# A two-layer encoder on one core: the output projection by blocks, its norm applied late, gates ahead of the next inputs

## The chip, the cores and the metric

The kernel runs as one program on 1 core of a Trainium2 chip. The metric is device time in microseconds (us). The kernel before took 3183.21 us, the median of 3 runs (3179.08 to 3185.33). Engines: PE (TensorE, matmuls), DVE (VectorE), ACT (ScalarE), POOL (GpSimd), SP (SyncE, which here only issues transfers between DRAM and the core's memory, SBUF). PE writes into PSUM banks.

## The reference

A hybrid encoder of two layers (model width 1024, feed-forward width 2816) over a prompt of 256 and a sample of 1024 tokens; 16 meta tokens precede each. All data are float32.

```python
def trunk(x, ...):
    h = concatenate([meta, x], axis=1)
    for layer in range(2):
        hn = rmsnorm(h, norm_mix_g[layer])
        if layer == 0: h = h + ab_layer(hn, ...)        # S5 and RG-LRU halves, concatenated, then @ w_out_ab
        else:          h = h + windowed_gqa(hn, ...)    # +-128 window, 16 heads, then @ w_o
        h = h + conv_ffn(rmsnorm(h, norm_ffn_g[layer]), w_up[layer], ..., w_down[layer])
    return rmsnorm(h, final_norm_g)[:, N_META:]

def conv_ffn(h, w_up, conv_w, conv_b, w_down):
    u = dwconv(h @ w_up, conv_w, conv_b, 1)             # centred, width 3
    a, g = u[..., :D_FF], u[..., D_FF:]
    return (gelu(g) * a) @ w_down
```

## The kernel before

Both sequences, 272 and 1040 tokens with their meta tokens, lie side by side as columns, with a few zero columns between; the 1024 features lie on the 128 partitions in KD = 8 blocks. A float32 matmul is made of three: each operand is split into a high part (`whi`, `hh`: an ACT cast) and the rest (`wlo`, `hl`: a subtraction on DVE or POOL), and `mm3` (L237 to L253) sums high by high, high by low and low by high over the 8 feature blocks. A weight block is `unit` (L226): one 512 KB load into a `raw` tile, the ACT cast, the subtraction.

Stages, in the order of the span: the mixer of layer 0 (to 488 us), `project_out(0)` (488 to 649), `ffn(0)` (649 to 1600), attention of layer 1 with its projections (1600 to 2112), `project_out(1)` (2112 to 2174), `ffn(1)` and the final norm (2174 to 3184).

`project_out` (L1481) works in 4 column chunks of 328 or 330 columns. In layer 0 it takes one chunk after the other and within it the 8 blocks m of output features: 24 matmuls over `hh` and `hl`, and extra matmuls with an identity (L252) that add the residual rows of x, which SP has loaded into `xr` tiles (up to 128 rows of 4 KB). The ACT copy puts the sum into `ha` (chunks 0, 1) or `hb` (2, 3). A chunk's columns of `od` (output of the mixer in DRAM) are staged (`stage`, L1441) through 3 buffers with the tag "t": load, ACT cast to `hh` (L1469), DVE subtraction to `hl` (L1470). Four weight units are kept. Then the norm of the chunk: `square` (8 squares on ACT, 7 adds on DVE at L272), `factors` (PE sums over partitions, L279), `spread` (DVE L289, PE L292), `apply` (8 scalar_tensor_tensor on DVE, L1503); for chunks 2 and 3 the result is stored to `ysp`. In layer 1 attention has handled the blocks of chunks 0 and 1 itself (`out_block`, L1428, over `hr` tiles, which share the tag "t"); at its end `rows(99)` stages everything that is left before the remaining blocks run.

`ffn` (L298) splits w_up into a Strassen-Winograd scheme of 7 products. The columns go in two halves (s = 0, 1). For pairs j of feature tiles PE runs 7 products of 12 matmuls (L427) with weights made of sums of `raw` tiles (POOL, L335) that are split again (ACT L361, POOL L362), and with inputs X1 to X7, sums of quarters of the normed columns (`inputs`, L370: DVE L382, L383, POOL L386, L387; splits at L1478 on ACT, L1479 on DVE). `follow` combines products on DVE (L438 to L449), `convolve` (L394) applies the depthwise taps, `gate` (L472) does gelu, product and split (`xa`, L477, L478). After two pairs, `down` (L490) multiplies by w_down (split at L486, L487; added into `hs` at L497). Between the halves the last pair's gates have to pass before `down` of that pair, and the inputs of the second half are made: here called the half-switch (1109 to 1160 us in layer 0, 2657 to 2690 in layer 1). The order of PE inside `ffn` is written out by hand (`run_pair`, orders SEVEN and TURNS); every other engine's order is set by a scheduler that follows priorities in program order and estimated readiness.

Of the kernel before, what the change touches and what calls it, by code (L numbers as in the profile page):

```python
# [89 lines left out]
class Trunk:  # L90
# [32 lines left out]
    def setup(self):  # L123
# [14 lines left out]
        self.ysp = self.dram.tile([128, KD, W - HALF], F32, tag="ysp", name="ysp")  # L138
# [116 lines left out]
    def norm(self, chunks, h):  # L255
# [4 lines left out]
        tile = lambda tag, n, b=1: p.tile([128, CH + 2], F32, tag=tag, name=tag, bufs=b)[:, :n]  # L260
        st = {}

        parts = lambda n: [min(x, n - 110) for x in range(0, n, 110)]

        def square(c):
            n = chunks[c][1]
            acc = st[c] = tile("acc", n)
            nc.scalar.activation(out=acc, in_=h(c, 0), func=AF.Square)
            for k in range(1, KD):
                sq = tile("t", n, 3)  # L270
                nc.scalar.activation(out=sq, in_=h(c, k), func=AF.Square)
# [26 lines left out]
    def ffn(self, l, p_norm, hn, h1, right):  # L298
# [9 lines left out]
        p_factors, p_spread, p_apply = p_norm  # L308
# [6 lines left out]
        order = lambda j: TURNS if turns(j) else SEVEN  # L315
# [54 lines left out]
        def inputs(first, ya, yb, n):  # L370
# [1327 lines left out]
```

## Time and profile before

| | |
|---|---|
| median of 3 runs | 3183.21 us (3179.08 to 3185.33) |
| the profiled execution | 3185.81 us, span 3184.0 us |
| PE busy | 2836.6 us (89%), 17944 matmuls |
| POOL, DVE, ACT busy | 1718.7 (54%), 2045.2 (64%), 1518.9 us (48%) |
| chain that ended last | PE 68%, DVE 13%, DMA 7%, ACT 4%, POOL 3%, issue 3% |

The span is the time from the first to the last instruction that the profile holds; the execution's own time is 1.81 us longer. In the strip of 40 slices PE stands at 9 in the long middle parts of both feed-forward stages and falls at the borders of stages: slices 7 to 8 (project_out(0), ffn(0) start), 14, 20, 26 to 28 and 33 to 34. The windows below take those borders one by one.

### The profile page before, as it was taken

Reading aid. Unit: us, or ns where it says so; the run is one execution under the profiler, and the core shown is the slowest. Engines: PE = TensorE matmul, PEld = TensorE weight load, DVE = VectorE, ACT = ScalarE, POOL = GpSimd, SP = SyncE. Lnnn points to the kernel's source line nnn. Section 1 sums busy time; section 2 is a strip of 40 time slices with the busy share of each in tenths; the row PEclk is TensorE's granted clock in tenths of the full one; section 3 lists DMA queues with packets and bytes.
Section 4 is the critical chain, followed back from the end, with each engine's and each line's share of the span. In section 5 each row is a group of like instructions: output and inputs, shape, how many; then the busy total and the mean of one; then the engine's idle time right before and its main releaser. Section 6 shows DMA issues by size and latency. Waiting matters only on the chain.

```text
span 3184.0 us, 48855 instructions
## 1 busy us (share of the span) xinstructions
PE 2836.6 (89%) x17944; PEld 2724.3 (86%) x17944; DVE 2045.2 (64%) x4215; ACT 1518.9 (48%) x2921; POOL 1718.7 (54%) x1446
## 2 busy tenths in 40 slices
PE   6999748869999979999979998866899997999996
PEld 5988537869999979999978887866799997899996
DVE  8998793365556685555664777656555556655664
ACT  5445772334444454444434666533444443544442
POOL 1000100078888887888604334316788887788881
PEclk9999878979999989999989999988899998999998
DMA  5322534433222242222237667663422222422221
GB/s 145 88 79 57 132 94 120 125 126 109 80 80 79 77 149 74 80 80 80 84 100 173 132 141 175 147 187 117 141 80 80 80 80 77 133 80 80 80 67 54
DMA packets 413438, 329.78 MB, mean 104 GB/s; under 512 B 39502, under 2 KB 388606, under 8 KB 413198
## 3 DMA queue, kind: packets, MB, share of 16 engines
q1 hardware_dynamic: 359086, 264.15, 28.8%
q0 software_dynamic: 35520, 32.89, 5.2%
q10 hardware_dynamic: 18592, 29.61, 2.7%
q8 instruction: 142, 2.33, 0.3%
q14 instruction: 98, 0.80, 0.1%
HBM read 261.96 MB, written 62.52 MB: 102 GB/s over the span
## 4 chain that ended last, share of the span: by engine, by line
PE 68%; DVE 13%; DMA 7%; ACT 4%; POOL 3%; issue 3%; SPq 1%; DVEq 0%; ACTq 0%; POOLq 0%
PE ps_a L427 9%; PE ps_c L427 9%; PE ps_d L427 9%; PE ps_b L427 5%; PE ps_a L248 4%; PE ps_a L253 4%; PE ps_a L249 4%; PE ps_c L248 2%; PE ps_c L253 2%; PE ps_c L249 2%; PE ps_b L248 2%; PE ps_b L253 2%; PE ps_d L248 2%; PE ps_d L253 2%; PE ps_b L249 2%
## 5 line engine op out<-in xcount | busy, mean ns | idle before, releaser
L487 POOL TENSOR_TENSOR dl<-rawd,dh 128x1024 fp32r<-128x1024 f32 x88 | 213.2, 2423 | 316.0 <-ACT dh L486 316.0
L248 PE MATMUL ps_a<-hh,whi 128*128 128x438 f32 (+5 forms) x848 | 295.7, 349 | 67.3 <-DVE hr L1438 29.9
L486 ACT CAST dh<-rawd 128x1024 fp32r<-128x1024 f32 x88 | 92.1, 1047 | 446.4 <-PE ps_d L249 425.3
L249 PE MATMUL ps_a<-hl,whi 128*128 128x438 f32 (+5 forms) x848 | 291.3, 344 | 1.9 <-DVE hl L1470 1.3
L253 PE MATMUL ps_a<-hh,wlo 128*128 128x438 f32 (+5 forms) x848 | 290.4, 343 | 0.0
L335 POOL TENSOR_TENSOR s<-raw 128x512 f32<-128x512 f32 x184 | 247.6, 1347 | 20.3 <-PE ps_d L253 14.8
L362 POOL TENSOR_TENSOR whi<-s,whi 128x512 fp32r<-128x512 f32 x176 | 234.2, 1341 | 27.6 <-ACT whi L361 27.5
L362 POOL TENSOR_TENSOR wlo<-s,wlo 128x512 fp32r<-128x512 f32 x176 | 234.1, 1331 | 12.5 <-ACT wlo L361 11.7
L248 PEld LDWEIGHTS ps_a<-hh,whi 128*128 128x128 f32 x848 | 165.8, 196 | 78.3 <-DVE hr L1438 30.1
L362 POOL TENSOR_TENSOR whi<-raw,whi 128x512 fp32r<-128x512 f32 x132 | 174.7, 1325 | 83.9 <-ACT whi L361 83.9
L361 ACT CAST wlo<-s 128x512 fp32r<-128x512 f32 x176 | 108.7, 620 | 231.8 <-PE ps_a L427 93.0
L427 PE MATMUL ps_a<-x,wlo 128*128 128x332 f32 (+1 forms) x1056 | 179.0, 319 | 41.6 <-POOL wlo L362 22.9
L427 PEld LDWEIGHTS ps_a<-x,wlo 128*128 128x128 f32 x1056 | 166.6, 192 | 43.0 <-POOL wlo L362 23.8
L427 PE MATMUL ps_d<-x,wlo 128*128 128x332 f32 (+1 forms) x1056 | 177.2, 317 | 6.9 <-ACT wlo L361 6.4
L427 PE MATMUL ps_a<-x,whi 128*128 128x332 f32 (+1 forms) x1056 | 177.8, 318 | 6.0 <-ACT u L436 6.0
L427 PE MATMUL ps_c<-x,wlo 128*128 128x332 f32 (+1 forms) x1056 | 178.4, 319 | 1.6 <-DVE t L443 1.6
L427 PE MATMUL ps_c<-x,whi 128*128 128x332 f32 (+1 forms) x1056 | 179.3, 320 | 0.0
L427 PE MATMUL ps_d<-x,whi 128*128 128x332 f32 (+1 forms) x1056 | 178.0, 318 | 0.0
L427 PEld LDWEIGHTS ps_a<-x,whi 128*128 128x128 f32 x1056 | 166.5, 191 | 6.5 <-ACT u L436 6.5
L362 POOL TENSOR_TENSOR wlo<-raw,wlo 128x512 fp32r<-128x512 f32 x132 | 172.0, 1321 | 0.0
L249 PEld LDWEIGHTS ps_a<-hl,whi 128*128 128x128 f32 x848 | 165.7, 195 | 7.4 <-DVE hl L1470 1.6
L427 PEld LDWEIGHTS ps_d<-x,wlo 128*128 128x128 f32 x1056 | 165.4, 190 | 7.6 <-ACT wlo L361 6.7
(499 smaller groups left out, 8872.9 us busy)
## 6 DMA issues: line engine op xcount, KB each, us to landing
raw<-in_w_up SPq DMA_DIRECT2D x176, 512.0 KB
rawd<-in_w_down SPq DMA_DIRECT2D x88, 512.0 KB
raw<-in_w_o SPq DMA_DIRECT2D x24, 512.0 KB
qs<-st SPq DMA_DIRECT2D x48, 219.0 KB
raw<-in_w_out_ab SPq DMA_DIRECT2D x20, 512.0 KB
q<-qs POOLq DMA_DIRECT2D x80, 128.0 KB, 3.8
hs<-hsp SPq DMA_DIRECT2D x6, 1312.0 KB
raw<-in_w_in_ab SPq DMA_DIRECT2D x12, 512.0 KB
```

The lines of the kernel that those rows point to most:

```text
L248: yield nc.tensor.matmul(ps, ah, bh, start=(j == 0), stop=False)
L249: yield nc.tensor.matmul(ps, ah, bl, start=False, stop=False)
L253: yield nc.tensor.matmul(ps, al, bh, start=False, stop=(j == n - 1))
L335: nc.gpsimd.tensor_tensor(out=out, in0=a, in1=b, op=op)
L361: nc.scalar.copy(w[:, 0], src)
L362: nc.gpsimd.tensor_tensor(out=w[:, 1], in0=src, in1=w[:, 0].bitcast(F32), op=ALU.subtract)
L427: nc.tensor.matmul(ps[b], w[:, e, k * 128:(k + 1) * 128], x[:, f, k, :n], start=(opens and k == 0 and y == 0), stop=(k == 3 and y == 2), s ...
L486: nc.scalar.copy(hi, raw)
L487: nc.gpsimd.tensor_tensor(out=lo, in0=raw, in1=hi.bitcast(F32), op=ALU.subtract)
```

## The change

1. `project_out`: in layer 0 chunks 0 and 1 still go one after the other; chunks 2 and 3 go as one group: each weight unit is used for chunk 2 and at once for chunk 3. Kept units come first. 4 fewer weight units are loaded and split in each layer (w_out_ab 20 to 16, w_o 24 to 20). `xr` has 6 buffers instead of 4, with the meta rows among them; `square` follows block by block.
2. Norm of chunks 2 and 3: the raw sums are spilled to `hsp`, `ysp` is gone; factors and spread run inside the first steps of `ffn`; chunk 2 is fetched and normed (8 DVE instructions) after the first pairs, chunk 3 at the half-switch.
3. Gates: the last pair of each half has the product order CLOSING; the DVE and ACT instructions of the next half's inputs are ordered behind the last gate's.
4. The two POOL additions of `inputs` move to DVE.
5. Weights: one of the four first w_up tiles is loaded during `project_out` into a tile of its own (`w1`); `follow` is not deferred in the first pairs.
6. Attention: `apply` of chunks 0 and 1 moves into the end of `ffn(0)`; at the end of attention two staged rows and 24 matmul steps alternate; tiles of the norm are 332 columns wide in parts of 111.

```diff
+CLOSING = (1, 6, 7, 2, 4, 5, 3)
...
-        order = lambda j: TURNS if turns(j) else SEVEN
+        order = lambda j: TURNS if turns(j) else CLOSING if j % len(up) == len(up) - 1 else SEVEN
...
-                raws[j] = [(wr if j % 2 else self.wraw).tile([128, 1024], F32, tag="raw", name="raw") for _ in range(2)]
+                raws[j] = [p.tile([128, 1024], F32, tag="raw", name="raw") for p in ((self.w1, wr) if j % 2 else (self.wraw,) * 2)]
...
+            def behind(ins, x):
+                if after:
+                    self.order(ins.ins, after[x])
...
             new(2, b21)
-            v.tensor_tensor(out=u, in0=b22, in1=b12, op=ALU.subtract)
-            v.tensor_tensor(out=w, in0=u, in1=b11, op=ALU.add)
+            if after:
+                normalize(3, yb, behind)
+            add(u, b22, b12, ALU.subtract)
+            add(w, u, b11, ALU.add)
             new(6, w)
             new(7, u)
-            nc.gpsimd.tensor_tensor(out=w, in0=b21, in1=w, op=ALU.subtract)
-            nc.gpsimd.tensor_tensor(out=u, in0=b12, in1=b11, op=ALU.subtract)
+            add(w, b21, w, ALU.subtract)
+            add(u, b12, b11, ALU.subtract)
...
+        def fetch(c):
+            t = xtile().rearrange("p a k n -> p (a k) n").bitcast(F32)
+            c0, n = NPC[c]
+            self.dma(t[:, :, :n], self.hsp[:, :, c0:c0 + n])
+            return t
+
+        def normalize(c, t, behind=lambda *x: None):
+            n = NPC[c][1]
+            for k in range(KD):
+                behind(v.scalar_tensor_tensor(out=t[:, k, :n], in0=t[:, k, :n], scalar=self.gn[:, 1 + 2 * l, k:k + 1],
+                                              in1=p_st[c], op0=ALU.mult, op1=ALU.mult), 1)
...
-            nc.scalar.copy(xh, g)
-            v.tensor_tensor(out=xl, in0=g, in1=xh.bitcast(F32), op=ALU.subtract)
+            gated[0] = nc.scalar.copy(xh, g).ins.name
+            gated[1] = v.tensor_tensor(out=xl, in0=g, in1=xh.bitcast(F32), op=ALU.subtract).ins.name
...
-                if i == 1 and not s:
-                    p_factors(3)
+                if not s and i < 2:
+                    (p_factors, p_spread)[i](2)
+                    (p_factors, p_spread)[i](3)
                 if i == 2:
-                    if not s:
-                        p_spread(3)
-                        p_apply(3)
...
-                    ya = xtile().rearrange("p a k n -> p (a k) n").bitcast(F32)
-                    self.dma(ya, self.ysp[:, :, 0:332])
+                    ya = fetch(2)
+                    normalize(2, ya)
...
-        down(end, cb, {6: [lambda: hfactors(2)]})
+        down(end, cb, {0: [lambda: apply(0)], 4: [lambda: apply(1)], 6: [lambda: hfactors(2)]})
...
-            rows(99)
+            while staged or todo or outs:
+                rows(2)
+                for _ in range(3 * KD):
+                    next(fill, None)
...
-        with tc.tile_pool(name="po", bufs=4) as p:
+        with tc.tile_pool(name="po", bufs=6) as p:
...
-            for c, (c0, n) in enumerate(PCH):
+            for group in ((2, 3),) if l else ((0,), (1,), (2, 3)):
+                rows = {c: [] for c in group}
+                for c in group if not l else ():
...
-                for j, m in enumerate([*range(4, 8), *range(4)] if c % 2 else range(8)):
+                for j, m in enumerate([*units, *(m for m in range(KD) if m not in units)]):
...
+                    for c in group:
+                        c0, n = PCH[c]
+                        s = slice(c0, c0 + n)
+                        ps = self.bank("abcd")
...
+                    pending += [(c, m) for c in group]
+                    if j >= start:
+                        for c, k in pending:
+                            square(c, [k])
+                        pending = []
...
-        square(3)
+            for c in (2, 3):
+                spill(c)
```

Lines of the kernel after are a few higher: L111 is L113, L121 is L123, L335 L339, L362 L366, L487 L517, L1479 L1505; the normalization of chunks 2 and 3 is L418, the four additions of `inputs` are L392.

The queue of SP in project_out(0), from the staged rows of chunk 1 on (`t<-od` is a staged block of 128 features, `xr` a tile of x rows, `raw` a weight unit). Before:

```order
L111 DMA t<-od 128x328 x5
L111 DMA xr<-in_x_sample 128x1024
L111 DMA xr<-in_x_sample 72x1024
L111 DMA xr<-in_x_sample 128x1024
L111 DMA raw<-in_w_out_ab 128x8x128 x4
L111 DMA t<-od 128x327 x5
L111 DMA xr<-in_x_sample 128x1024
L111 DMA xr<-in_x_sample 71x1024
L111 DMA raw<-in_w_out_ab 128x8x128 x2
```

After, from the x rows of chunk 1 on:

```order
L113 DMA xr<-in_x_sample 128x1024 x2
L113 DMA t<-od 128x328 x3
L113 DMA xr<-in_x_sample 72x1024
L113 DMA t<-od 128x328 x2
L113 DMA raw<-in_w_out_ab 128x8x128 x4
L113 DMA xr<-in_x_sample 128x1024 x2
L113 DMA xr<-in_x_sample 71x1024
L113 DMA t<-od 128x328 x5
L113 DMA t<-od 128x327 x5
L113 DMA raw<-in_w_out_ab 128x8x128 x2
```

The staged blocks of chunk 1 stand behind the x rows of chunk 1 instead of ahead of those of chunk 2; the x rows of chunks 2 and 3 come together, and all ten staged blocks of these chunks behind them.

The queue of POOL at the start of ffn(0) (`s` is a sum of weight tiles, `x` an input sum). Before:

```order
L362 TENSOR_TENSOR whi<-raw,whi 128x512
L197 TENSOR_TENSOR rs<-rs,mhalf 110x4
L362 TENSOR_TENSOR whi<-raw,whi 128x512
L335 TENSOR_TENSOR s_5685<-raw 128x512
L335 TENSOR_TENSOR s_5697<-raw 128x512
L335 TENSOR_TENSOR s_5685<-s_5685,raw 128x512
L335 TENSOR_TENSOR s_5691<-raw 128x512
L335 TENSOR_TENSOR s_5691<-s_5691,raw 128x512
L386 TENSOR_TENSOR x<-ha,x 128x4x330
L362 TENSOR_TENSOR wlo<-raw,wlo 128x512 x2
L387 TENSOR_TENSOR x<-ha 128x4x330
```

After:

```order
L366 TENSOR_TENSOR whi<-raw,whi 128x512
L366 TENSOR_TENSOR wlo<-raw,wlo 128x512
L366 TENSOR_TENSOR whi<-raw,whi 128x512
L366 TENSOR_TENSOR wlo<-raw,wlo 128x512
L339 TENSOR_TENSOR s_5648<-raw 128x512
L339 TENSOR_TENSOR s_5660<-raw 128x512
L339 TENSOR_TENSOR s_5648<-s_5648,raw 128x512
L339 TENSOR_TENSOR s_5654<-raw 128x512
L339 TENSOR_TENSOR s_5654<-s_5654,raw 128x512
L366 TENSOR_TENSOR whi<-s_5648,whi 128x512
L366 TENSOR_TENSOR whi<-s_5660,whi 128x512
```

Four weight splits stand ahead of the first sum instead of two, the two additions into `x` are gone, and the low half from `raw` has moved from the tenth row to the second.

The queue of DVE at the half-switch of ffn(0) (`xa` is the gate's low part, `hs` takes the blocks of `down`). Before:

```order
L398 SCALAR_TENSOR_TENSOR t<-ps_b,cw_655,t 128x328
L398 SCALAR_TENSOR_TENSOR t<-ps_c,cw_655,t 128x328 x2
L1479 TENSOR_TENSOR x<-x 128x1328 x3
L398 SCALAR_TENSOR_TENSOR t<-ps_d,cw_655,t 128x328
L475 TENSOR_TENSOR ps_b<-ps_b,a 128x328
L475 TENSOR_TENSOR ps_c<-ps_c,a 128x328
L398 SCALAR_TENSOR_TENSOR t<-ps_d,cw_655,t 128x328
L478 TENSOR_TENSOR xa<-ps_b,xa 128x328
L478 TENSOR_TENSOR xa<-ps_c,xa 128x328
L475 TENSOR_TENSOR ps_d<-ps_d,a 128x328
L478 TENSOR_TENSOR xa<-ps_d,xa 128x328
L497 TENSOR_TENSOR hs<-hs,ps_a 128x328
```

After:

```order
L527 TENSOR_TENSOR hs<-hs,ps_b 128x328
L527 TENSOR_TENSOR hs<-hs,ps_c 128x328
L505 TENSOR_TENSOR ps_d<-ps_d,a 128x328
L527 TENSOR_TENSOR hs<-hs,ps_d 128x328
L276 TENSOR_TENSOR acc<-acc,t 128x328
L527 TENSOR_TENSOR hs<-hs,ps_a 128x328
L276 TENSOR_TENSOR acc<-acc,t 128x328
L508 TENSOR_TENSOR xa<-ps_d,xa 128x328
L418 SCALAR_TENSOR_TENSOR x<-x,vec,y 128x331 x8
L527 TENSOR_TENSOR hs<-hs,ps_b 128x328
L1505 TENSOR_TENSOR x<-x 128x1328
L527 TENSOR_TENSOR hs<-hs,ps_c 128x328
```

Before, three splits of inputs stand ahead of three of the gates; after, the eight multiplications of chunk 3 (L418) and the splits (L1505) come behind the last gate (`xa<-ps_d`), and blocks of `down` already stand ahead of it.

## Rows read from the trace of the kernel before

**Rows 1.** Windows by stage; columns are in its first row.
```profile
core 0: us, PE busy (x) PEld busy (x) DVE busy (x) ACT busy (x) POOL busy (x), PEclk, DMA share, GB/s
599.00:649.00 50.00, 37.86 (x257) 37.59 (x256) 11.75 (x19) 11.03 (x19) 3.53 (x3) 0.86 0.31 100
649.00:722.00 73.00, 38.95 (x206) 37.04 (x205) 49.31 (x54) 30.44 (x51) 60.17 (x37) 0.76 0.49 154
722.00:1109.00 387.00, 386.77 (x2531) 386.77 (x2532) 231.52 (x483) 178.28 (x323) 317.39 (x235) 0.99 0.28 82
1109.00:1160.00 51.00, 33.58 (x209) 32.44 (x208) 42.76 (x60) 29.03 (x48) 35.59 (x17) 0.83 0.32 101
2053.00:2112.00 59.00, 29.12 (x173) 27.58 (x173) 23.18 (x42) 15.76 (x28) 13.25 (x20) 0.74 0.66 192
2174.00:2265.00 91.00, 48.44 (x275) 45.64 (x273) 61.93 (x75) 39.49 (x66) 79.42 (x52) 0.77 0.50 159
2640.00:2730.00 90.00, 64.94 (x393) 61.78 (x393) 58.58 (x97) 41.04 (x78) 59.82 (x40) 0.87 0.31 100
```

**Rows 2.** Waits of PE: what was waited for, us in total, times, longest us.
```profile
PE ps_a L248 <- ACT xa L477: 34.7, 4, 14.2
```

**Rows 3.** Timeline of PE: start, us, engine, line, op, [idle before <-releaser].
```profile
617.00 0.49 PE L252 MATMUL ps_a<-ident,xr 71*128 71x71 f32 x1 [12.14 <-DMA xr<-in_x_sample]
...
1596.68 0.64 PE L248 MATMUL ps_a<-xa,dh 128*128 128x328 f32 x1 [5.18 <-ACT xa L477]
...
2097.09 0.64 PE L248 MATMUL ps_a<-hh,whi 128*128 128x328 f32 x1 [29.88 <-DVE hr L1438]
...
2670.13 0.64 PE L248 MATMUL ps_a<-xa,dh 128*128 128x328 f32 x1 [12.51 <-ACT xa L477]
```

**Rows 4.** Chain of waits in project_out(0): start us, us, what.
```profile
490.02 10.77 DMA xr<-in_x_sample
...
598.91 18.04 DMA xr<-in_x_sample
```

**Rows 5.** Timeline of SP (it issues DMAs), project_out(0) and attention's end.
```profile
547.70 8.20 SPq L111 DMA_DIRECT2D t<-od  x5
...
598.48 0.69 SPq L111 DMA_DIRECT2D xr<-in_x_sample  x2
...
2093.39 0.58 SPq L111 DMA_DIRECT2D hr<-hsp  x1
```

**Rows 6.** Timeline of DVE: staging, half-switch, attention's end, ffn(1) start.
```profile
559.84 1.32 DVE L1470 TENSOR_TENSOR hl<-t,hh 128x328 fp32r<-128x328 f32 x3
...
1113.56 1.53 DVE L1479 TENSOR_TENSOR x<-x,x 128x1328 fp32r<-128x1328 f32 x1
...
1129.69 8.66 DVE L1479 TENSOR_TENSOR x<-x 128x1328 fp32r<-128x1328 f32 x3
...
2060.83 2.34 DVE L1464 TENSOR_TENSOR t<-t,y 128x328 f32<-128x328 f32 x1 [0.22 <-DMA y<-rs]
...
2079.74 0.50 DVE L1464 TENSOR_TENSOR t<-t,y 128x327 f32<-128x327 f32 x1 [8.91 <-DMA t<-od]
...
2096.96 0.49 DVE L1470 TENSOR_TENSOR hl<-t,hh 128x328 fp32r<-128x328 f32 x1
...
2170.50 3.88 DVE L1503 SCALAR_TENSOR_TENSOR hb<-hb,vec,y 128x331 f32<-128x331 f32 x8 [0.25 <-ACT y L294]
...
2222.26 8.45 DVE L1503 SCALAR_TENSOR_TENSOR hb<-hb,vec,y 128x328 f32<-128x328 f32 x8
```

**Rows 7.** Timeline of POOL at the start of ffn(1).
```profile
2174.86 3.81 POOL L335 TENSOR_TENSOR s<-raw 128x512 f32<-128x512 f32 x2 [6.53 <-PE ps_d L253]
...
2191.12 3.97 POOL L386 TENSOR_TENSOR x<-ha,x 128x1320 f32<-128x1320 f32 x1 [1.47 <-DVE x L1479]
...
2197.57 3.22 POOL L387 TENSOR_TENSOR x<-ha 128x1320 f32<-128x1320 f32 x1
...
2256.47 2.51 POOL L362 TENSOR_TENSOR whi<-raw,whi 128x512 fp32r<-128x512 f32 x2
```

More of the change, by code (lines that the diff above doesn't have):

```diff
@@ L368, in xtile, with inputs @@
             return xs.tile([128, 2, 4, 332], FR, tag="x", name="x")
-        def inputs(first, ya, yb, n):
+        def inputs(first, ya, yb, n, after=None):
             b11, b21, b12, b22 = ya[:, 0:4], ya[:, 4:8], yb[:, 0:4], yb[:, 4:8]
@@ L504, in ffn @@
         hn.close()
-        wr, xs = (left.enter_context(tc.tile_pool(name=x, bufs=b)) for x, b in (("wr", 2), ("xs", 7)))
+        wr, xs = (left.enter_context(tc.tile_pool(name=x, bufs=b)) for x, b in (("wr", 1), ("xs", 7)))
         sp, tp = pool(left, "ss"), pool(left, "tp")
@@ L518, in give @@
                 square(c)
+        h1.close()
+        wp, ap, hp = (pool(right, x, side=RIGHT) for x in ("wd", "ap", "hs"))
         load_raw(0)
@@ L1337, in attention @@
         factors, spread, apply = norm
-        for step in ((apply, 0), v, v, (apply, 1), v, (first, 8), v, (first, 0), (spread, 2), (apply, 2), v,
+        for step in (v, v, v, (first, 8), v, (first, 0), (spread, 2), (apply, 2), v,
                      (factors, 3), v, (spread, 3), (apply, 3), *[v] * 6, (first, 1)):
@@ L1444, in stage @@
         nc = self.nc
-        get = lambda tag, b: self.nrm.tile([128, CH + 2], F32, tag=tag, name=tag, bufs=b)
+        get = lambda tag, b: self.nrm.tile([128, 332 if tag == "y" else CH + 2], F32, tag=tag, name=tag, bufs=b)
         c0, n = chunk
@@ L1521, in project_out @@
[L1521 to L1537 removed]
+            behind = {(1,): {1: [(factors, 0)], 3: [(spread, 0)], 4: [(apply, 0)]},
+                      (2, 3): {0: [(factors, 1)], 1: [(spread, 1)], 2: [(apply, 1)]}}
@@ new lines, in project_out @@
+            start = 0
+        else:
+            behind = {(2, 3): {0: [(square, 0)], 1: [(factors, 0), (square, 1)], 2: [(spread, 0), (factors, 1)], 3: [(apply, 0), (spread, 1)],
+                               4: [(apply, 1)]}}
+            start = 2
+        units, pending = {}, []
+        with tc.tile_pool(name="po", bufs=6) as p:
+            if l:
+                for c, (c0, n) in enumerate(PCH):
+                    a = HALF if c == 2 else c0
+                    t, x = hv(a, c0 + n - a)
+                    nc.gpsimd.dma_start(out=t[:, :, x:x + c0 + n - a], in_=self.hsp[:, :, a:c0 + n])
+            else:
+                meta = p.tile([128, D], F32, tag="xr", name="xr")
+                self.dma(meta[:NM], self.i["meta_tokens"])
+            for group in ((2, 3),) if l else ((0,), (1,), (2, 3)):
+                rows = {c: [] for c in group}
+                for c in group if not l else ():
+                    c0, n = PCH[c]
```

130 lines of the change are left out of this document (54 added, 76 removed).

## Prediction

> **What bounds the kernel now.** I read the windows by stage first, then the waits of PE, then the timelines at the waits. The reader is to see in the windows that the body of a feed-forward stage is PE and nothing else: 2531 matmuls in 387 us, 0.153 us each, with clock 0.99 [rows 1]. At 0.153 us the matmuls of the other windows explain only a part of their length: 31.5 of 73 us at the start of ffn(0), 32 of 51 at its half-switch, 42 of 91 at the start of ffn(1), 60 of 90 at its half-switch, 26.5 of 59 at the end of attention, 39 of 50 in the last chunk of project_out(0) [rows 1]. These borders lose 41.5 + 19 + 49 + 30 + 32.5 + 11 = 183 us, and the change lies in them; what it does to the bodies is nothing, as the matmuls are the same. The waits name losers: 34.7 us in four waits for the gate's `xa` [rows 2], 29.88 in one for `hr` [rows 3]. Clock falls to 0.76 and 0.77 in the two starts [rows 1], so a wait there also costs slower matmuls after it. All sums are made against the profiled execution, 3185.8 us (span 3184.0); the median of 3183.2 lies 2.6 below it and takes the same sum.
>
> **project_out(0): a loss.** Today the staged blocks of a chunk are loaded while the chunk before still has blocks to run: the five of chunk 1 take from 547.70 to 561.16, that is 13.5 us, all hidden [rows 5, 6]. What is not hidden is the x rows: PE stands 12.14 us for the load of 71 rows, which takes 18.04 us [rows 3, 4]. After the change the staged blocks stand behind the x rows in SP's queue and share three buffers with the squares, so they begin about when their chunk is needed. For one chunk PE has 33 matmuls (by its order) before it needs the last staged feature, 5 us against 13.5: +8.5. For chunks 2 and 3 ten blocks take 27 us, and PE has some 58 matmuls, 9 us: 18 us in place of the 12.1, and the 18.04 us load runs beside the staging. The mixer in front loses five subtractions of 0.44 us [rows 6], 2.2 us. Sum +8.5 + 18 - 12.1 - 2.2 = +12. Bounds: -14 if all staging is hidden (only the 12.1 and 2.2 count); at the rate of staging at the end of attention, ten blocks in 36.6 us (2060.83 to 2097.45 [rows 6]), and behind the 18.04 us load, it is 13 + 45 - 14 = +44. I take +12, since the 13.5 us were measured in this stage. Behind a waiting block on PE stand all later blocks; ACT and DVE have nothing else to do there (11 and 12 us busy of 50 [rows 1]), so it is paid in full.
>
> The two loads of 41 and 71 rows took 10.77 and 18.04 us [rows 4], 0.26 and 0.25 us per row of 4 KB: the time goes by rows, as if one engine moved them. The Trainium skill, "DMA: Bandwidth & Descriptors", section "Why a DMA increments its semaphore by 16 and not by 1", says that a transfer is spread over the largest number of engines up to 16 that divides its slowest dimension, which for 41 and 71 is one. By that rule the trace agrees, and the 71 rows cost the same 18 us after the change; no more buffers make them shorter, only earlier.
>
> **Starts of the feed-forward stages.** POOL is the bound: at ffn(1) it is busy 79.4 of 91 us [rows 1] and its chain from the end of project_out (2174.86) to the last split of the first two pairs (2258.98) is 84 us [rows 7]. Out of this chain go the two additions, 3.97 + 3.22 = 7.2 us [rows 7]; two more splits, of 1.26 us each (half of 2.51), run before the end of project_out: 2.5 us; and the eight multiplications of chunk 3, which took 8.45 us there and 3.88 just before [rows 6], leave the start, which I count as the difference, 4.6. Sum -14 for each start, -28 for both. In the first wait PE has 48 matmuls of the early pair to run, 7.3 us. The two additions land on DVE at 1.53 to 2.89 us (the split of the same size alone, and a third of 8.66 [rows 6]); DVE is busy 62 of 91 us [rows 1], so I count nothing; without that cover up to +6 per start. Bounds: 0 (POOL only waits elsewhere, for the `raw` tile that is still loaded late) to -41 and -49, all that the windows lose. With about a third of the waiting gone, a third of the slow matmuls goes: PE is busy 39 us for 31.5 and 48.4 for 42 [rows 1], 14 us too many in both; -6, between 0 and -14.
>
> **Half-switches.** Of the 34.7 us, the longest wait, 14.2, is that of ffn(0) [rows 2]; that of ffn(1) is 12.51, and at the end of ffn(0), where no next inputs are made, it is 5.18 [rows 3]. Ahead of the gates stand three splits, 8.66 us [rows 6]. Ordered gates should leave 5.2: -9 in ffn(0) and -7 in ffn(1). But the eight multiplications of chunk 3 come here, 3.9 to 8.5 us, and the four additions all on DVE, 1.5 to 2.9 each; behind them on DVE wait the additions of `down` into `hs`, which free PE's banks, and in ffn(0) the squares for which the next norm's matmuls wait. I charge 5 us in ffn(0) and 1 in ffn(1), which has no squares: -4 and -6. Bounds: -14 and -12 (the waits gone) to +6 and +5 (contended rates, all in front of `down`).
>
> DVE's eight multiplications take 0.49 us each with POOL idle and 1.06 beside its sums and splits, the split of x 1.53 and 2.89 [rows 6]. The Trainium skill, "SBUF — State Buffer", section "Who interferes with whom", says that a DVE instruction with two SBUF inputs and a GpSimd instruction that reads SBUF shut each other out for the whole instruction. The trace agrees in size. The rule speaks against this change: by it the work added here would run at the second rates, 8 x 1.06 + 4 x 2.89 = 20 us instead of 10, and the half-switches would give 0.
>
> **Attention and the rest.** At its end `hr` is first issued at 2093.39, after the staging, and PE stands 29.88 us until 2097.09 [rows 3, 5]; the four blocks left, 24 matmuls or 3.7 us each, then run to 2112. After the change they alternate, but use the same three buffers: 15 turns instead of 10. Without its one long wait (8.91 us [rows 6]) one of the ten turns in 36.6 us took 2.8 us, so 42 us from 2060.8: 2103, -9; at 3.7 us a turn it is 2116, +4. I take -8; bounds -15 (the four blocks wholly hidden) to +4. At its start 16 multiplications, 7.8 us at 0.49, leave DVE's path; half of it was awaited: -4, between 0 and -8. The eight weight units less are hidden by PE: 0, or -2. CLOSING at the ends of the stages: 0.
>
> **Sum.** +12 - 28 - 6 - 4 - 6 - 8 - 4 = -44: 3185.8 - 44 = 3141.8, and from the median 3139 us.
>
> **Rivals.**
> 1. The starts stay with the `raw` loads and ACT, the additions slow DVE as the contended rows say: starts -12 with their clock, half-switches 0, attention -8 in all, project_out +12: -8, 3175 us. For it: the chain on POOL begins only at the end of project_out, after 6.53 us of waiting for PE [rows 7], and that the change keeps. Against: POOL's 79 of 91 busy. Chance 0.17.
> 2. More comes back: most of the waits at the starts close and with them the low clock (-55 for both), half-switches -15, attention -15, project_out +5: -80, 3103 us. For it: 183 us are lost at the borders. Against: POOL still has about 70 us of work per start, against 42 of PE. Chance 0.15.
> 3. Slower: the three staging buffers become the bound. In project_out(0) every staged block waits behind the x rows and turns at the rate seen at the end of attention, +44, and there the `hr` tiles with store and load hold a buffer about 9 us, five rounds of it +10 instead of -8. With the rest (-28 - 6 - 4 - 6 - 4 = -48) this is +6, 3189 us. It decides from 50 us of staging beyond today's. For it: the 36.6 us of ten blocks. Against: 13.5 us for five in the very stage. Chance 0.10.
> 4. The norms applied late only move: each piece taken from the starts is paid at the half-switch, project_out as summed, 3183 us within a few. Against: additions to a chain off POOL do not come back. Chance 0.04.
>
> The forecast keeps 0.54; its own range is 3122 to 3158. For 8 in 10 the range goes to 3108 and 3178: beyond lie half of rival 2 and rivals 3 and 4. About 0.2%, 6 us, is what a measurement of this kernel can tell from no change. Faster by more: forecast, rivals 1 (most of it) and 2: 0.85. Within: 0.06. Slower: 0.09.
>
> **What would show it.** In the changed profile: PE waits for `hh` or `hl` of staged blocks at both chunk borders of project_out(0), 26 us in all, and none for x rows; POOL's chain at the starts about 70 us, its waits for `wlo` under 8 us each; one wait for `xa` per half-switch near 5 us; no wait near 30 us at the end of attention, but several of 2 to 6. I am wrong if staging waits exceed 50 us, if the starts are still 70 and 90 us long, or if `down` at the half-switch stands for DVE's additions.

## The result, and the profile after

The changed kernel takes 3128.22 us (median of 4 runs, 3126.86 to 3131.19) against 3184.27 (4 runs, 3179.08 to 3186.29) of the kernel before on the same chip: ratio 0.9828, 95% interval 0.9811 to 0.9845. The profiled execution is 3128.57 us, its span 3126.6 us, against 3185.81 and 3184.0. The gain is 56 us where 44 were forecast.

I divide both spans at the same landmarks (the first matmul of a stage, the first `down` that comes in the steady rhythm of a feed-forward stage, the last value product of attention) and subtract. In the column of the forecast the -6 for the clock is divided between the two starts, and the -2.2 of project_out(0) stands at the mixer:

| part | before, us | after, us | difference | forecast |
|---|---|---|---|---|
| up to the end of the mixer | 487.4 | 486.8 | -0.6 | -2.2 |
| project_out(0) | 161.7 | 176.6 | +14.8 | +14.2 |
| start of ffn(0) | 84.8 | 73.0 | -11.8 | -17 |
| half-switch of ffn(0) | 108.3 | 107.7 | -0.7 | -4 |
| end of ffn(0), start of attention | 54.7 | 45.9 | -8.8 | -4 |
| end of attention, project_out(1) | 115.1 | 100.2 | -14.9 | -8 |
| start of ffn(1) | 92.2 | 72.7 | -19.5 | -17 |
| half-switch of ffn(1) | 118.4 | 110.1 | -8.3 | -6 |
| end of the kernel | 57.9 | 55.3 | -2.6 | 0 |
| the four bodies of ffn, body of attention | | | -5.5, +0.7 | 0 |

So the change acts at the borders, as forecast, and every sign there is right. The sizes at the half-switches, at the two ends of attention and, less so, at the two starts are not, and the bodies, put at 0, gave 5.5 us. The windows of the kernel after for the two starts and the end of attention (columns as in [rows 1]):

```profile
663.30:736.30 73.00, 52.30 (x278) 49.82 (x278) 61.51 (x67) 34.15 (x56) 66.29 (x41) 0.79 0.49 153
2150.60:2223.30 72.70, 51.59 (x279) 50.08 (x278) 61.21 (x68) 34.73 (x57) 67.79 (x42) 0.77 0.50 157
2050.40:2150.60 100.20, 83.18 (x531) 81.75 (x532) 56.26 (x100) 31.79 (x58) 20.16 (x26) 0.90 0.56 169
```

and of the kernel before between the same landmarks:

```profile
649.10:733.90 84.80, 50.53 (x266) 48.61 (x266) 56.15 (x67) 36.29 (x62) 71.12 (x44) 0.76 0.48 149
2174.60:2266.80 92.20, 49.63 (x277) 46.83 (x276) 61.83 (x75) 39.49 (x66) 81.15 (x53) 0.76 0.50 158
2059.50:2174.60 115.10, 83.08 (x547) 82.24 (x548) 61.98 (x111) 33.95 (x57) 17.53 (x25) 0.87 0.59 172
```

Length less PE's busy time is what PE stands: in the starts 34.3 and 42.6 us before, 20.7 and 21.1 after. A matmul there takes as long as before (52.30/278 = 0.188 us against 50.53/266 = 0.190; 0.185 against 0.179): the granted clock stays at 0.79 and 0.77, and the 6 us that I expected from it did not come.

The largest waits of PE that the change touches (waited for: us in total, times, longest):

```profile
PE ps_c L283 <- DVE acc L276: 23.1, 7, 9.2
PE ps_a L249 <- ACT hh L1495: 21.9, 2, 17.9
PE ps_c L296 <- DVE t L293: 19.6, 5, 7.0
PE ps_b L249 <- ACT whi L234: 12.3, 1, 12.3
...
PE ps_a L249 <- ACT xa L507: 1.1, 2, 0.8
```

The 34.7 us for ACT's `xa` [rows 2] have become 1.1, and the one wait of 29.88 us for `hr` [rows 3] is gone. In their place stand staged blocks (`hh`, 4.01 + 17.93 us in project_out(0)), the squares and factors of norms (`acc`, `t`), and one weight unit of `w_o` (`whi`). The timeline of PE has them one by one:

```profile
535.20 0.64 PE L249 MATMUL ps_a<-hh,whi 128*128 128x328 f32 x1 [4.01 <-ACT hh L1495]
...
592.54 0.64 PE L249 MATMUL ps_a<-hh,whi 128*128 128x328 f32 x1 [17.93 <-ACT hh L1495]
...
687.32 3.09 PE L296 MATMUL ps_c<-t,ones 111*128 111x111 f32 x12 [6.85 <-DVE t L293]
...
1146.09 1.28 PE L283 MATMUL ps_c<-ones,acc 128*111 128x1 f32 x6 [9.23 <-DVE acc L276]
...
2075.57 0.64 PE L249 MATMUL ps_b<-hh,whi 128*128 128x328 f32 x1 [12.32 <-ACT whi L234]
```

### The profile page after: what moved, and what is told of

Same layout as the page of the kernel before. It is cut to its first block, busy times and chain, and to the rows that moved or that the text cites. A ratio compares the mean times of both kernels' runs of the same rounds, so it can differ in the third digit from the quotient of the medians.

```text
span 3126.6 us, 48771 instructions
## 1 busy us (share of the span) xinstructions
PE 2829.9 (91%) x17936; PEld 2716.1 (87%) x17936; DVE 2045.8 (65%) x4213; ACT 1509.8 (48%) x2913; POOL 1698.5 (54%) x1438
## 4 chain that ended last, share of the span: by engine, by line
PE 69%; DVE 16%; DMA 7%; ACT 4%; issue 3%; POOL 1%; SPq 1%; DVEq 0%; ACTq 0%; POOLq 0%
PE ps_d L457 9%; PE ps_c L457 9%; PE ps_a L457 9%; PE ps_b L457 5%; PE ps_a L249 4%; PE ps_a L254 4%; PE ps_a L250 4%; PE ps_c L249 2%; PE ps_c L254 2%; PE ps_c L250 2%; PE ps_b L254 2%; PE ps_b L249 2%; PE ps_d L249 2%; PE ps_d L254 2%; PE ps_b L250 2%
## 5 line engine op out<-in xcount | busy, mean ns | idle before, releaser
L517 POOL TENSOR_TENSOR dl<-rawd,dh 128x1024 fp32r<-128x1024 f32 x88 | 213.2, 2423 | 299.0 <-ACT dh L516 299.0
L339 POOL TENSOR_TENSOR s<-raw 128x512 f32<-128x512 f32 x184 | 251.9, 1370 | 28.1 <-PE ps_d L254 25.5
L366 POOL TENSOR_TENSOR wlo<-s,wlo 128x512 fp32r<-128x512 f32 x176 | 233.7, 1329 | 18.6 <-ACT wlo L365 16.0
L366 POOL TENSOR_TENSOR whi<-s,whi 128x512 fp32r<-128x512 f32 x176 | 231.3, 1324 | 18.1 <-ACT whi L365 18.1
L366 POOL TENSOR_TENSOR whi<-raw,whi 128x512 fp32r<-128x512 f32 x132 | 177.3, 1344 | 68.2 <-ACT whi L365 68.2
L457 PE MATMUL ps_c<-x,wlo 128*128 128x330 f32 (+1 forms) x1152 | 192.5, 316 | 0.0
L457 PE MATMUL ps_a<-x,whi 128*128 128x330 f32 (+1 forms) x1104 | 187.2, 319 | 1.3 <-ACT u L466 1.3
L457 PE MATMUL ps_d<-x,whi 128*128 128x330 f32 (+1 forms) x1104 | 182.9, 314 | 0.0
L457 PE MATMUL ps_d<-x,wlo 128*128 128x330 f32 (+1 forms) x1008 | 171.4, 320 | 12.2 <-DVE ps_b L475 6.5
L457 PEld LDWEIGHTS ps_c<-x,wlo 128*128 128x128 f32 x1152 | 180.1, 191 | 0.0
L457 PEld LDWEIGHTS ps_a<-x,whi 128*128 128x128 f32 x1104 | 175.1, 193 | 1.8 <-ACT u L466 1.6
L457 PE MATMUL ps_a<-x,wlo 128*128 128x330 f32 (+1 forms) x1008 | 169.7, 318 | 4.5 <-ACT u L466 4.5
L366 POOL TENSOR_TENSOR wlo<-raw,wlo 128x512 fp32r<-128x512 f32 x132 | 172.3, 1319 | 0.7 <-ACT wlo L365 0.5
L457 PEld LDWEIGHTS ps_d<-x,wlo 128*128 128x128 f32 x1008 | 158.7, 192 | 14.9 <-DVE ps_b L475 7.1
L254 PEld LDWEIGHTS ps_a<-hh,wlo 128*128 128x128 f32 x848 | 166.0, 196 | 6.4 <-issue 3.0
```

Of the source, the lines that this page charges most:

```text
L254: yield nc.tensor.matmul(ps, al, bh, start=False, stop=(j == n - 1))
L339: nc.gpsimd.tensor_tensor(out=out, in0=a, in1=b, op=op)
L366: nc.gpsimd.tensor_tensor(out=w[:, 1], in0=src, in1=w[:, 0].bitcast(F32), op=ALU.subtract)
L457: nc.tensor.matmul(ps[b], w[:, e, k * 128:(k + 1) * 128], x[:, f, k, :n], start=(opens and k == 0 and y == 0), stop=(k == 3 and y == 2), s ...
L517: nc.gpsimd.tensor_tensor(out=lo, in0=raw, in1=hi.bitcast(F32), op=ALU.subtract)
```

## The experiments

All ratios are to the kernel before, measured beside each experiment; the changed kernel itself has 0.9828, and 0.001 is 3.2 us. The intervals reach about 0.0017 to either side, so that a difference of less than some 8 us between two versions is not clear of noise by the whole alone (an estimate from these intervals). Each experiment alters the changed kernel.

### project_out(0): why its second half waits 18 us

**The three staging buffers.** Chunks 2 and 3 go one after the other, so that PE needs five staged blocks and not ten. The squares of both stay beside chunk 3, and the norm of chunk 1 moves by some steps (that part of the edit is left out here).

```diff
-            for group in ((2, 3),) if l else ((0,), (1,), (2, 3)):
+            for group in ((2, 3),) if l else ((0,), (1,), (2,), (3,)):
...
-                    pending += [(c, m) for c in group]
+                    pending += [(c, m) for c in {(2,): (), (3,): (2, 3)}.get(group, group)]
```

> The changed kernel, but in layer 0 chunks 2 and 3 one after the other again (squares of both beside chunk 3, norm still late). The changed kernel waits 17.9 us for staged blocks ahead of the pair of chunks. My theory: the wait is the ten staged blocks that come late, since the block-wise squares hold the three buffers; with chunk 2 alone in front only five have to come, and those of chunk 3 hide behind chunk 2: project_out(0) shorter by 9 to 11 us, 3117 to 3121. Rival: it is the 71-row load in front of the staging; then the wait moves to the x rows of chunk 3 as before the change and the time stays within 4 of 3128.

3129.36 us, ratio 0.9828 (0.9809 to 0.9848): no difference. PE's timeline shows the wait unchanged:

```profile
595.60 0.64 PE L249 MATMUL ps_a<-hh,whi 128*128 128x328 f32 x1 [18.16 <-ACT hh L1495]
```

So my reason in the prediction, ten blocks that take 27 us through three buffers, falls. The x rows of chunk 3, the 71 among them, stand ahead of the staged blocks of chunk 2 here too: SP issues three x-row tiles from 574.57 on and the staged blocks from 575.83 on. The trace of the changed kernel says what PE waits for. SP's queue, and the chain of waits for the same DMA:

```profile
571.74 1.16 SPq L113 DMA_DIRECT2D xr<-in_x_sample  x3
573.01 27.20 SPq L113 DMA_DIRECT2D t<-od  x10
```

```profile
573.01 19.00 DMA t<-od
```

The first staged block is issued at 573.01, right behind the three x-row tiles, the last of them with 71 rows, and lands 19.00 us later. The strip of DMA over 565 to 600 us (40 cells of 0.875 us; tenths of the 16 engines, then GB/s) shows 12 cells with 23 to 29 GB/s and less than a tenth of the engines:

```profile
DMA  0000000066999999994000000000000007931774
GB/s 0 0 0 0 0 0 0 0 51 215 323 375 306 380 388 374 361 380 170 28 25 26 29 25 25 25 26 29 25 23 25 8 0 189 273 114 16 223 194 145
```

**The x rows, cut.** Each load of x rows whose row number is no multiple of 16 is made as two: 41 as 32 + 9, 72 as 64 + 8, 71 as 64 + 7.

```diff
-                            self.dma(xr[:m], x[0, t - col - NM:t - col - NM + m])
+                            for r0, r1 in ((0, m // 16 * 16), (m // 16 * 16, m)):
+                                if r0 < r1:
+                                    self.dma(xr[r0:r1], x[0, t - col - NM + r0:t - col - NM + r1])
```

> The changed kernel with each load of x rows whose count is no multiple of 16 cut in two (41 into 32 and 9, 72 into 64 and 8, 71 into 64 and 7). After e5 my first theory (ten staged blocks, and the three buffers) fell: with five blocks the wait was the same. New theory: the load of 71 rows runs as on one DMA engine for 18 us, and the staged loads issued behind it on the same queue wait for it there, since each has a share on that engine; the first staged load lands 19 us after its issue. Cut in two, it is short, and the 17.9 us wait shrinks to 3 to 6 (the staged loads by themselves): minus 12 to 15 us, 3113 to 3117. Rival: the staged loads are slow by themselves, 13.5 us for five as in the kernel before; then the wait stays above 10 and the time falls by less than 6.

3120.79 us, ratio 0.9801 (0.9785 to 0.9817), some 9 us below the changed kernel; project_out(0) is 12 us shorter up to the first matmul of ffn(0) (160.6 against 172.9 from its first x-row matmul). PE's wait and the chain of waits:

```profile
578.28 0.64 PE L249 MATMUL ps_a<-hh,whi 128*128 128x328 f32 x1 [6.60 <-ACT hh L1495]
```

```profile
570.29 7.45 DMA t<-od
```

The staged blocks and their buffers are the same; the loads of x rows alone are different (the 64 rows now stand in front of the first staged blocks, the 7 behind three of them), and the first block lands in 7.45 us instead of 19.00. The wait of 3.52 us for the 41 rows at the start of the stage is gone too. That the long load holds the blocks issued behind it is shown. That it does so because one DMA engine carries all 71 rows and the next load needs that engine too fits the strip, and is argued.

**Staging first.** The staged blocks of the next group are issued before the blocks of the current one, ahead of the x rows.

```diff
-                    if c:
-                        self.stage(self.od, (c0, n), [k for k in range(KD) if k not in STAY], False)
+                for c in {(0,): (1,), (1,): (2, 3)}.get(group, ()) if not l else ():
+                    self.stage(self.od, PCH[c], [k for k in range(KD) if k not in STAY], False)
```

> The changed kernel with the staging of the next chunks issued before the blocks of the current chunk. My theory: their loads then stand ahead of the squares for the three buffers and run beside the blocks; the waits of 4.0 and 17.9 us for staged blocks go: minus 16 to 22 us, 3106 to 3112. Rival: the transfers themselves are the bound, above all the 71 x rows that need 18 us; then PE waits 8 to 12 us for x rows in their place: 3118 to 3124.

3120.19 us, ratio 0.9792 (0.9774 to 0.9809), some 11 us less. No wait for staged blocks is left, but the wait for the rows themselves is back, as in [rows 3, 4]. PE's timeline, and the chain of waits:

```profile
584.72 0.70 PE L253 MATMUL ps_b<-ident,xr 71*128 71x71 f32 x2 [11.51 <-DMA xr<-in_x_sample]
```

```profile
565.45 19.22 DMA xr<-in_x_sample
```

**Both.** The last two edits together.

> Both together: staging of the next chunks issued before the blocks of the current one (e6), and the x rows cut in two (e9). Theory: both waits of project_out(0), that for staged blocks and the 11.5 us one for x rows which took its place in e6, are gone; project_out(0) from 157 us in e6 to 145, the kernel at 3104 to 3109. Rival: x rows and staged blocks together are bound by the transfers; then one wait of 5 us or more stays, and 3111 to 3116.

3104.97 us, ratio 0.9750 (0.9731 to 0.9769): 23 us below the changed kernel, 80 below the one before. Over project_out(0) PE is busy 143.10 of 144.70 us, with no wait over 1.7:

```profile
492.40:637.10 144.70, 143.10 (x925) 138.99 (x926) 43.35 (x71) 44.86 (x89) 8.26 (x11) 0.93 0.39 120
```

Both causes had to go: each edit alone leaves the other's wait.

### The starts of the feed-forward stages

**The last two additions back on POOL**, without an order.

```diff
-            add(w, b21, w, ALU.subtract)
-            add(u, b12, b11, ALU.subtract)
+            nc.gpsimd.tensor_tensor(out=w, in0=b21, in1=w, op=ALU.subtract)
+            nc.gpsimd.tensor_tensor(out=u, in0=b12, in1=b11, op=ALU.subtract)
```

> The changed kernel with the last two additions of the inputs back on POOL, without an order behind the gates. My theory: POOL's chain is the bound of both starts, so each start grows by about the two additions, 7 us, and the half-switches by 0 to 4 each: 3142 to 3150. Rival 1: DVE, with the additions on it, is the bound of the starts; then the time stays or falls by up to 6. Rival 2: the starts are bound by the late weight tile; then it stays within 3.

3149.60 us, ratio 0.9883 (0.9867 to 0.9899), 17 us more: the starts +2.4 and +6.0, the half-switches +2.0 and +3.3. At ffn(1) that is near the 7 us expected, at ffn(0) a third of it. The whole is the more robust number; single stages of two runs differ by 1 to 3 us.

**No early w_up tile**: all are loaded as before.

```diff
-                raws[j] = [p.tile([128, 1024], F32, tag="raw", name="raw") for p in ((self.w1, wr) if j % 2 else (self.wraw,) * 2)]
+                raws[j] = [p.tile([128, 1024], F32, tag="raw", name="raw") for p in ((wr, wr) if j % 2 else (self.wraw,) * 2)]
...
-        wr, xs = (left.enter_context(tc.tile_pool(name=x, bufs=b)) for x, b in (("wr", 1), ("xs", 7)))
+        wr, xs = (left.enter_context(tc.tile_pool(name=x, bufs=b)) for x, b in (("wr", 2), ("xs", 7)))
```

> The changed kernel without the one w_up tile that is loaded during project_out: both tiles of the second pair come after its end, as before the change. My theory (POOL's chain): two splits fewer run ahead, the starts grow by 2 to 4 us each: 3132 to 3136. Rival: the early tile is the main cause of the shorter starts, as without it PE has nothing to run while POOL makes the first sums: 8 to 12 us each, 3144 to 3152.

3139.26 us, ratio 0.9855 (0.9836 to 0.9875), 8 us more; the starts are 76.2 and 77.4 us, +3.2 and +4.7.

**Norm factors later**: factors and spread of chunks 2 and 3 in the second pair of steps.

```diff
-                if not s and i < 2:
-                    (p_factors, p_spread)[i](2)
-                    (p_factors, p_spread)[i](3)
...
+                if f0 == 2 and not s:
+                    behind = {1: [lambda: p_factors(2), lambda: p_factors(3)], 3: [lambda: p_spread(2)], 4: [lambda: p_spread(3)]}
```

> The changed kernel with factors and spread of chunks 2 and 3 moved from the first two steps of each ffn into its second pair. At the start of ffn PE now waits 4.5 and 6.9 us (layer 0), 3.2, 2.7, 7.0 and 1.3 us (layer 1) for the squares and the diagonal of these norms. Theory of the prediction (POOL's chain is the bound of the starts): PE waits for weights instead, the starts fall by 0 to 4 us each, 3120 to 3128. Rival (PE's own order is the bound): minus 8 to 12 each, 3104 to 3112.

3135.51 us, ratio 0.9842 (0.9826 to 0.9859), 4 us more and so not clear of noise; neither the gain of my theory nor that of the rival came. The waits for `acc` and `t` fall from 23.1 and 19.6 us to 13.4 and 10.5, yet the starts get no shorter. Windows of both starts in this kernel:

```profile
664.50:738.10 73.60, 52.52 (x277) 48.21 (x277) 54.10 (x66) 35.20 (x58) 71.63 (x43) 0.84 0.50 152
2155.90:2231.10 75.20, 51.87 (x277) 48.70 (x277) 55.68 (x67) 35.44 (x58) 71.98 (x44) 0.82 0.49 152
```

POOL is busy 71.63 of 73.6 us: with most of PE's norm waits out of the starts, its chain is what is left to end last. All three runs fit POOL's chain as the bound of the starts.

### The half-switches

**No order behind the gates.**

```diff
-                if after:
-                    self.order(ins.ins, after[x])
+                pass
```

> The changed kernel without the order of the next inputs behind the last gate (the product order CLOSING stays). My theory: splits stand ahead of the gates on DVE again, a wait for xa of 10 to 14 us comes back at both half-switches, but the inputs are ready earlier: +3 to +6 in ffn(0), where the gates were not what ended the switch, +8 in ffn(1): 3139 to 3143. Rival: the gain of 9 us in ffn(1) came from CLOSING or from the additions on DVE; then within 3 of 3128.

3166.65 us, ratio 0.9935 (0.9920 to 0.9949), 34 us more, over twice the 11 to 15 us of my theory, and the rival gave none; the half-switches are +10.3 and +21.3. PE's and DVE's timelines in ffn(0) show why (in this kernel L474 is the addition in `follow` that takes a product out of PE's bank `ps_d`, L417 the multiplications of chunk 3):

```profile
1134.26 3.67 PE L456 MATMUL ps_d<-x,wlo 128*128 128x330 f32 x12 [11.48 <-DVE ps_b L474]
...
1158.62 0.64 PE L249 MATMUL ps_a<-xa,dh 128*128 128x328 f32 x1 [7.86 <-ACT xa L506]
```

```profile
1122.32 6.08 DVE L417 SCALAR_TENSOR_TENSOR x<-x,vec,y 128x331 f32<-128x331 f32 x4
...
1128.80 4.52 DVE L417 SCALAR_TENSOR_TENSOR x<-x,vec,y 128x331 f32<-128x331 f32 x4
...
1133.71 0.49 DVE L474 TENSOR_TENSOR ps_b<-ps_d,t 128x330 f32<-128x330 f32 x1
```

Without the order the scheduler puts all eight multiplications, 10.6 us, ahead of one addition of 0.49 us, and PE waits 11.48 us for it before it writes `ps_d` again. That the order is worth more in the changed kernel than it would have been before, since the change itself brought these multiplications to this place, is argued; no run tries the order in the kernel before.

**The old product order in the last pair.**

```diff
-        order = lambda j: TURNS if turns(j) else CLOSING if j % len(up) == len(up) - 1 else SEVEN
+        order = lambda j: TURNS if turns(j) else SEVEN
```

> The changed kernel with the old product order SEVEN for the last pair of each half. My theory: CLOSING is worth 1 to 3 us at each of the four ends of a half, as only two instead of three combinations are left after the last product: 3132 to 3138. Rival: it is worth nothing since the gate's own chain is the wait: 3126 to 3130.

3140.18 us, ratio 0.9853 (0.9837 to 0.9870), 8 us more: +1.7 and +2.6 at the half-switches, +2.5 at the end of ffn(0), +1.9 at the end of the kernel. The waits for `xa` are 15.0 us in 4, between the 34.7 of before [rows 2] and the 1.1 of the changed kernel.

**Norm factors of the next half later**, so that PE need not wait 9.23 us for the squares of the last chunk.

```diff
-        down(end, cb, {} if last else {4: [lambda: hfactors(0)]})
+        down(end, cb)
...
-behind = {1: [lambda: hfactors(1)],
+behind = {0: [lambda: hfactors(0)], 1: [lambda: hfactors(1)],
```

> The changed kernel with the matmuls of the next norm's factors of quarter 0 moved from the last down of the first half into the second pair of the second half. At the half-switch of ffn(0) PE waits 9.2 us there for the last addition of the squares. My theory: this wait takes the place of the gate's, and it is all that kept the half-switch of ffn(0) from giving what that of ffn(1) gave: minus 5 to 9 us, 3119 to 3123. Rival: DVE's chain (chunk 3's norm, four additions, six splits) ends last, so that PE waits for an input instead: minus 0 to 3.

3133.75 us, ratio 0.9831 (0.9806 to 0.9855): no gain in the whole. In the profiled execution (3145.16 us, 11 above the median) the half-switch of ffn(0) is 5 us longer, but that of ffn(1), which the edit does not touch, is 3.5 longer too. The 9.23 us are gone, and PE waits for the next things that DVE makes:

```profile
1154.86 0.64 PE L457 MATMUL ps_b<-x,whi 128*128 128x332 f32 x1 [3.39 <-ACT x L1504]
...
1205.88 1.59 PE L296 MATMUL ps_c<-t,ones 111*128 111x111 f32 x6 [6.95 <-DVE t L293]
```

There DVE's chain ends last, whichever of its results PE asks for first.

### The end of attention, and all together

**All staged rows first**, then the matmul steps.

```diff
-            while staged or todo or outs:
-                rows(2)
-                for _ in range(3 * KD):
-                    next(fill, None)
+            rows(99)
```

> The changed kernel with one part undone: at the end of attention everything is staged first and the four blocks that are left come after it. My theory: the alternation is what moved the stretch from the last attention matmul to the first of ffn(1) from 117.8 to 103.0 us; undone, PE gets one long wait of 20 to 30 us for hr back, and the time goes up by 10 to 15 us, to 3138 to 3143. Rival: the stretch got shorter because project_out(1) splits four weight units less and leaves the norm of chunks 2 and 3 to ffn(1); then undoing the alternation costs at most 4 us.

3141.94 us, ratio 0.9858 (0.9843 to 0.9873), 10 us more. The end of attention takes 106.3 us, against 100.2 in the changed kernel and 98 to 104 in the other experiments. The wait on PE there is then

```profile
2085.93 0.64 PE L249 MATMUL ps_b<-hh,whi 128*128 128x328 f32 x1 [19.09 <-ACT whi L234]
```

and not the 29.88 us of [rows 3]. Alternating is thus worth 10 us by the whole and 2 to 8 by the stage; the rest of the 14.9 is left for what changed beside it (fewer weight units, the late norm). How it divides among these stays open.

**The two edits of project_out(0) and the late factors.**

> e10 and e11 together, the version meant to beat both kernels: 3098 to 3108 if the starts are bound by POOL, 3085 to 3095 if by the place of the norm's matmuls.

3107.84 us, ratio 0.9756 (0.9741 to 0.9770): the same as without the late factors (0.9750). The best version is the one with staged blocks first and the rows cut.

## Why the prediction was right, and where it was not

**project_out(0): right size by luck, wrong cause.** +12 was forecast, +14.2 came (with the mixer), and the waits for staged blocks are the 4.01 + 17.93 = 22 us of the 26 expected. The step that failed is "the 18.04 us load runs beside the staging". It runs ahead of it: the first block issued behind it landed after 19.00 us, and neither the ten blocks nor the three buffers count (sequential chunks change nothing, cut rows take 12 us off). That the 18 us put down to ten blocks came as 17.93 is luck. The +8.5 for chunk 1 came as 4.0, and waits that the sum left out made up for it: 3.52 us for the 41 rows, 0.45 before, and 1.66 + 1.56 for squares. That I had weighed buffer turns alone hid that the loss could be had back in two lines. One detail was also misread: the five blocks loaded from 547.70 [rows 5], the first row of SP's queue before, are chunk 2's; chunk 1's had been staged in the mixer.

The prediction read the two row loads by the rule in the Trainium skill, "DMA: Bandwidth & Descriptors", section "Why a DMA increments its semaphore by 16 and not by 1". The strip agrees (25 GB/s, under a tenth of the engines), and by the same rule 64 rows can be spread over 16 engines: cut that way the rows no longer hold up the blocks.

**Starts: right bound, half the reason.** -28 without the clock was forecast, -31.3 came, and three runs fit POOL as the bound. At ffn(0) POOL's chain itself, from the first sum to the last split of the first two pairs, shrank from 91.0 us to 79.2, by as much as the start, 11.8. POOL's timeline before, then after:

```profile
649.36 2.62 POOL L335 TENSOR_TENSOR s<-raw 128x512 f32<-128x512 f32 x1 [8.26 <-PE ps_d L253]
...
737.75 2.56 POOL L362 TENSOR_TENSOR whi<-raw,whi 128x512 fp32r<-128x512 f32 x2
```

```profile
663.57 2.63 POOL L339 TENSOR_TENSOR s<-raw 128x512 f32<-128x512 f32 x1 [14.56 <-PE ps_d L254]
...
740.20 2.56 POOL L366 TENSOR_TENSOR whi<-raw,whi 128x512 fp32r<-128x512 f32 x2
```

At ffn(1) it shrank from 84.1 us [rows 7] to 77.6 (2150.87 to 2228.47), 6.5. Forecast were 14 at each, down to about 70 us:

```profile
2150.87 3.83 POOL L339 TENSOR_TENSOR s<-raw 128x512 f32<-128x512 f32 x2 [10.98 <-PE ps_d L254]
...
2192.68 2.42 POOL L517 TENSOR_TENSOR dl<-rawd,dh 128x1024 fp32r<-128x1024 f32 x1
...
2203.28 2.59 POOL L517 TENSOR_TENSOR dl<-rawd,dh 128x1024 fp32r<-128x1024 f32 x1
...
2225.93 2.54 POOL L366 TENSOR_TENSOR whi<-raw,whi 128x512 fp32r<-128x512 f32 x2
```

It now holds two `dl` splits of 2.42 and 2.59 us, of which before one stood inside it and one behind. They are of the part I left out: `w_down`. Before, its load stood in SP's queue behind six w_up loads, and PE waited 1.86 + 5.45 + 4.29 = 11.6 us for `dh` and `dl` when the first `down` came. SP's and PE's timelines of the kernel before:

```profile
2174.80 46.02 SPq L111 DMA_DIRECT2D raw<-in_w_up  x6
...
2240.06 1.93 SPq L111 DMA_DIRECT2D rawd<-in_w_down  x1
```

```profile
2253.72 0.64 PE L253 MATMUL ps_a<-xa,dl 128*128 128x328 f32 x1 [1.86 <-POOL dl L487]
...
2259.81 0.64 PE L248 MATMUL ps_a<-xa,dh 128*128 128x328 f32 x1 [5.45 <-ACT dh L486]
...
2265.01 0.64 PE L253 MATMUL ps_a<-xa,dl 128*128 128x328 f32 x1 [4.29 <-POOL dl L487]
```

After, it stands behind two, and PE has no such wait. SP's timeline of the kernel after:

```profile
2150.82 16.88 SPq L113 DMA_DIRECT2D raw<-in_w_up  x2
...
2178.50 2.35 SPq L113 DMA_DIRECT2D rawd<-in_w_down  x1
```

So of the -19.5 at ffn(1) 4.0 lie ahead of the first `down` (76.7 us before, 72.7 after) and 15.5 behind its start, 11.6 of them these waits. That the two starts together come near the forecast is thus in part luck. What brought `w_down` forward stays open. It is not the early w_up tile: in the run without it the load is issued 25.6 us after the start of ffn(1), against 27.9 in the changed kernel and 65.5 before, and PE has no such wait. SP's timeline of that run:

```profile
2183.99 4.42 SPq L113 DMA_DIRECT2D rawd<-in_w_down  x1
```

The clock term of -6 failed: fewer waits, but as slow matmuls. Its own working, a third of 14 us, gives 5 and not 6.

**Half-switches: the waits for `xa` went, and in ffn(0) others came.** Forecast were 5 us left of `xa` at each; 1.1 are left in all, for the gates run first. The 5 us charged for DVE in ffn(0) were too little: PE stands 9.23 us for the squares, behind multiplications, splits and additions on DVE:

```profile
1132.10 3.87 DVE L418 SCALAR_TENSOR_TENSOR x<-x,vec,y 128x331 f32<-128x331 f32 x8
...
1144.73 1.30 DVE L276 TENSOR_TENSOR acc<-acc,t 128x328 f32<-128x328 f32 x3
...
1152.88 5.42 DVE L392 TENSOR_TENSOR x<-x 128x1328 f32<-128x1328 f32 x1
```

So -4 was mis-sized by 3.3; ffn(1), which has no squares, gave 8.3 where 6 were forecast.

The rule on DVE and GpSimd in the Trainium skill, "SBUF — State Buffer", section "Who interferes with whom", was to bring the half-switches to 0. These rows say that the multiplications met no contention there (3.87 us for eight, as in the quiet row of 3.88 [rows 6]); one addition of four did, 5.42 us against 1.53. POOL stood idle for 16.46 us meanwhile, waiting for a factor of the norm. In the start of ffn(1), beside POOL's sums, the eight of chunk 2 took 10.97 us on DVE. POOL's timeline of the kernel after, then DVE's:

```profile
1147.87 5.39 POOL L198 TENSOR_TENSOR rs<-rs,mhalf 111x3 f32<-111x3 f32 x1 [16.46 <-DVE rs L197]
...
2195.27 10.97 DVE L418 SCALAR_TENSOR_TENSOR x<-x,vec,y 128x332 f32<-128x332 f32 x8 [0.98 <-DMA x<-hsp]
```

Nothing in these rows speaks against the rule; the work met POOL less often than I charged it.

**Attention: sign right, size half.** -12 was forecast, -23.7 came. At its end the terms were drawn from buffer turns (2.8 or 3.7 us each), but PE no longer waits for turns: one wait of 12.32 us for a unit of `w_o` is left, and the blocks that did wait before now run among the rows. At its start I took half of the 7.8 us of multiplications, -4. Before, the first matmul of attention waited 4.39 us for its `hh`; this wait is gone, which is that size, though no run undoes the move alone. The rest of the 8.8 us in this stretch goes with the wait for `xa` at the end of ffn(0), 5.18 us before [rows 3] and 0.77 after. PE's timeline before, then after:

```profile
1618.33 0.45 PE L1176 MATMUL ps_a<-whi,hh 128*128 128x256 f32 x1 [4.39 <-ACT hh L599]
```

```profile
1594.53 0.41 PE L249 MATMUL ps_a<-xa,dh 128*128 128x328 f32 x1 [0.77 <-ACT xa L507]
```

CLOSING, put at 0 for the ends of the stages, is worth 2.5 us there and 1.9 at the end of the kernel, by the run with the old order, in which the wait for `xa` is 5.41 us again.

**The rivals.** That the starts stay, that the norms only move, and that the staging makes the whole slower are out by the table. "More comes back" had its mechanism in part: the waits at the starts closed by half, but the clock did not follow.

## What to carry to other kernels

Look at what stands ahead in the queue before you count buffers: here a load of 71 rows held up every load issued behind it, and cutting it took two lines. Put what PE waits for ahead of what only prepares the next stage, and say so to the scheduler: 0.5 us of addition behind 10 us of preparation cost PE the 10. When a chain is shortened at a border, list the second and third thing that PE needs there (here `w_down`); 11.6 us of the gain were theirs.

## What the runs showed of the hardware

- A load of 71 rows of 4 KB was followed by a load over 128 partitions that landed after 19.00 us; with the rows cut as 64 + 7 it landed after 7.45. While the 71 rows ran alone the DMA moved 23 to 29 GB/s, against 306 to 388 in the busy cells before.
- In the starts the granted clock stayed at 0.76 to 0.79 though PE stood 41.8 us there instead of 76.9; with the norm factors moved out it was 0.84 and 0.82, and the stage was not shorter.
- Eight scalar_tensor_tensor instructions of 128 x 331 took 3.87 us on DVE in a half-switch and 10.97 (128 x 332) beside POOL's sums of weights.
